# A hybrid gMLP and Mamba-2 layer on one core: small parameters, last sums, late squares and inverse roots emitted elsewhere

## The chip, the cores and the metric

One core of a Trainium2 chip. TensorE (PE) multiplies matrices into eight PSUM banks; VectorE (DVE), ScalarE (ACT) and GpSimd (POOL) do the elementwise work; the SP queue issues the loads and ACT's queue the stores. The metric is the device time of one execution in microseconds, as the median of several runs.

## The reference

One layer (DEPTH 1, batch 1, 1024 tokens, width 1024) in float32:

```python
mod = jax.nn.silu(c) @ ada_w + ada_b
shift, scale, gate = jnp.split(mod, 3, axis=-1)
h = rms_norm(x, norm_w) * (1 + scale[:, None, :]) + shift[:, None, :]
proj = h @ w_in
gm_u, gm_v, gm_z, ssm_z, xbc, dt_raw, g_a, g_b = jnp.split(proj, SPLITS, axis=-1)
y_a = spatial_gating(gelu(gm_u), gelu(gm_v), gm_ln_w, gm_ln_b, gm_ws, gm_bs) * silu(gm_z)
xbc = silu(causal_depthwise_conv(xbc, conv_w, conv_b))
xs, bm, cm = jnp.split(xbc, (SSM_D_INNER, SSM_D_INNER + SSM_GROUPS * SSM_STATE), axis=-1)
dt = softplus(dt_raw + dt_bias)
a = -jnp.exp(a_log)
y_b = ssd_scan(xs, dt, a, bm, cm) + xh * d_skip[:, None]
yz = (y_b * silu(ssm_z)).reshape(b, s, 8, 256)
y_b = rms_norm(yz, ssm_norm_w per group)
merged = sigmoid(g_a) * (y_a @ w_proj_a) + sigmoid(g_b) * (y_b @ w_proj_b)
x = x + gate * (merged @ w_out)
return rms_norm(x, final_norm_w)
```

The `rms_norm` of `yz` is what the change works on most: for each of 8 groups and 1024 tokens, the inverse root of the mean of 256 squares.

## The kernel before

**Precision and products.** Each float32 operand is split into a high part (a cast to fp32r, on ACT) and a low part (the rest, a subtraction on VectorE, names ending in l), and a product is three matmuls: high by high, high by low, low by high. The large products use a scheme with seven products of sums of blocks instead of eight (names p1 to p7; t1 to t4 and s1 to s4 are the sums).

**Stages.** 0 to 76 us: the modulation vector (`pm`, matrix-vector products with `aw` in eight steps), h (transposes `px`, then `hf`, `b11` ... `t4`) and first products (`acc`), steps n = 1 to 7 side by side. 75 to 153 us: the v projection (`v_block`), 28 units of 12 matmuls (2.72 us each). 153 to 955 us: the other columns of the in-projection in pairs (names ending in cb, uz, x, g, z), with convolution and gates. 955 to 1145 us: the SSD in four rounds of two groups (0 and 1, 2 and 3, and so on) with four steps of two chunks each, filled up with the matmuls of proj_a (`pma`, eight output blocks dd). 1157 to 1318 us: proj_b, in units p1, p3, p6, p5, p7, p2, p4 with eight k each. Then the out projection.

**Order.** Instructions under `pin` stay in program order on their engine; the others are placed by the framework's scheduler. `later(delay, f, ...)` puts a piece of work into a list, and `run_tasks` emits it that many slots on, a slot being about a product. Tiles share slots by tag: a `w4` slot (`wide`) is taken over once the tile before it has been read for the last time, and SP, like every engine, takes its instructions in order.

**Small parameters.** `late_loads` (L235) loads convolution weights and norm weights into `pkb` (five loads on SP); after product 12 of step n = 4 `small_parameters` (L453) transposes it on PE into `pp1` and copies the result on VectorE into `par2` and `cwt`, and `dsk` into `dskt`. `cwt` is first used at L1029, at 167.87 us.

**Last sums.** `last_sums` (L325) forms the sums t1, t3, t2, t4 of the last k block of h in slots 7 to 9 of step 7; `last_split` (L154) splits them for the products. PE's first operand of the v projection, `p1v0h`, is cast on ACT behind `t1h`.

**Squares and roots.** In each group the gated output `yz` is squared on ACT for the two halves q of the tokens (four chunks each), `post2` (L1222) sums the squares over channels by matmuls with `ones` (`pq`), writes mean + eps into `ssq` on VectorE and, for q = 1, takes the power -0.5 on POOL for that group; `post3` (L1237) transposes the group's roots on PE, copies them to a row (the tiles `cwt` and `tri` are used again for it) and stores them in `rs_d`, from where they come back to all partitions as `rb`. In proj_b VectorE forms `yn` = `yn` x weight x `rb` (L1535) and splits it into the operands `p1bh`, `p1bl`, `p3bh` and so on. For the last round's groups 6 and 7 and q = 1 the two squared tiles are kept (`late`), and their sums (`y0p`, `y1p`) and transposes (`y2p`, `y3p`) stand between the units k = 1, 2 and k = 4, 6 of p1, in PSUM banks that p3 takes over.

**Weights of proj_a.** `wa_block` (L1319) makes `wah` (ACT) and `wal` (VectorE) of the next block dd + 1 after k = 1 of a block.

## Time and profile before

| what | us |
|---|---|
| runs | 1399.33, 1403.52, 1399.36 (median 1399.36) |
| profiled execution, its own time | 1403.59 |
| its span | 1401.9 |
| PE busy / VectorE / ACT / POOL | 1372.1 / 1044.2 / 802.1 / 187.1 |

The page gives the span in 40 slices; a digit is the busy share of a slice in tenths, PEclk the granted clock of PE:

```profile
PE   8899999999999999999999999999999999999998
DVE  4676876777778789688888786388767755859976
ACT  5564566666656665465576565587766723223443
POOL 1000000000000000000000000028878840000002
PEclk9999999999999999999999999999999999999999
```

A row of the timeline has start, duration, engine, line, operation, out<-in, shapes, count and, in brackets, the idle time before it with what ended it. A row of the waits has the engine that waited, its line, what it waited for, and then total us, times and the longest. A row of windows has the stretch, its length, busy us of PE, PE's weight load, VectorE, ACT and POOL, then the granted clock, the DMA share and GB/s.

### The profile page before, as it was taken

Reading aid. Unit: us, or ns where it says so; the run is one execution under the profiler, and the core shown is the slowest. Engines: PE = TensorE matmul, PEld = TensorE weight load, DVE = VectorE, ACT = ScalarE, POOL = GpSimd, SP = SyncE. Lnnn points to the kernel's source line nnn. Section 1 sums busy time; section 2 is a strip of 40 time slices with the busy share of each in tenths; the row PEclk is TensorE's granted clock in tenths of the full one; section 3 lists DMA queues with packets and bytes.
Section 4 is the critical chain, followed back from the end, with each engine's and each line's share of the span. In section 5 each row is a group of like instructions: output and inputs, shape, how many; then the busy total and the mean of one; then the engine's idle time right before and its main releaser. Section 6 shows DMA issues by size and latency. Waiting matters only on the chain.

```text
span 1401.9 us, 20221 instructions
## 1 busy us (share of the span) xinstructions
PE 1372.1 (98%) x6967; PEld 1136.7 (81%) x6967; DVE 1044.2 (74%) x1725; ACT 802.1 (57%) x1447; POOL 187.1 (13%) x188
## 2 busy tenths in 40 slices
PE   8899999999999999999999999999999999999998
PEld 7578888888888888888888888888888887888886
DVE  4676876777778789688888786388767755859976
ACT  5564566666656665465576565587766723223443
POOL 1000000000000000000000000028878840000002
PEclk9999999999999999999999999999999999999999
DMA  8575533333344667786665765598777746978913
GB/s 264 164 233 153 150 120 106 105 121 120 110 131 139 199 191 238 228 265 208 199 210 169 242 217 165 169 350 310 280 255 272 279 162 240 346 251 306 384 64 120
DMA packets 247227, 288.60 MB, mean 206 GB/s; under 512 B 14508, under 2 KB 194132, under 8 KB 247124
## 3 DMA queue, kind: packets, MB, share of 16 engines
q1 hardware_dynamic: 173716, 203.76, 45.0%
q10 hardware_dynamic: 73408, 83.54, 17.6%
q8 instruction: 55, 0.90, 0.3%
q14 instruction: 48, 0.39, 0.1%
HBM read 199.79 MB, written 87.46 MB: 205 GB/s over the span
## 4 chain that ended last, share of the span: by engine, by line
PE 81%; DMA 8%; DVE 4%; ACT 3%; issue 1%; SPq 1%; POOL 1%; ACTq 0%; POOLq 0%; DVEq 0%
PE xz L571 6%; PE xx L571 6%; PE xcb L571 6%; PE xuz L571 5%; PE xg L571 5%; PE ox L1783 3%; PE yp L1597 3%; PE ycb L571 3%; PE yz L571 3%; DMA dcy<-acs_d 3%; PE vx L960 3%; PE yx L571 3%; PE pma L81 3%; PE yg L571 3%; PE yuz L571 3%; PE zz L571 2%
## 5 line engine op out<-in xcount | busy, mean ns | idle before, releaser
L1113 POOL TENSOR_SCALAR_AFFINE_SELECT dcy<-dcy 128x1024 f32<-128x1024 f32 x32 | 35.0, 1094 | 799.3 <-DMA yl<-ya_d 752.0
L1118 ACT ACTIVATE dcy<-dcy,nacs 128x128 f32<-128x128 f32 x256 | 78.5, 389 | 14.9 <-POOL dcy L1113 14.4
L1110 ACT ACTIVATE ea<-dcy 64x512 f32<-64x512 f32 x64 | 40.1, 626 | 14.3 <-DMA dcy<-acs_d 13.9
L1535 DVE SCALAR_TENSOR_TENSOR yn<-yn,par,rb 128x512 f32<-128x512 f32 x32 | 23.9, 747 | 27.5 <-DMA yn<-yb_d 27.5
L81 PE MATMUL pma<-yh,wah 128*128 128x512 f32 x128 | 43.9, 424 | 0.0
L81 PE MATMUL pma<-yh,wal 128*128 128x512 f32 x128 | 42.7, 415 | 0.0
L1138 DVE TENSOR_TENSOR dcy<-dcy,pc 128x1024 f32<-128x1024 f32 x32 | 38.9, 1217 | 4.9 <-PE pc L84 4.3
L1198 DVE TENSOR_TENSOR ym<-yn,ea 128x512 f32<-128x512 f32 (+1 forms) x32 | 19.9, 622 | 29.8 <-PE yn L81 29.6
L1200 POOL TENSOR_TENSOR yz<-y,sl 128x512 f32<-128x512 f32 x32 | 41.4, 1292 | 1.1
L81 PE MATMUL pma<-yl,wah 128*128 128x512 f32 x128 | 40.5, 398 | 0.0
L1033 ACT ACTIVATE ac<-ac 128x1024 f32<-128x1024 f32 x32 | 33.9, 1060 | 9.7 <-DVE ac L1031 9.5
L1199 POOL TENSOR_TENSOR y<-y,ym 128x512 f32<-128x512 f32 (+1 forms) x32 | 36.6, 1142 | 15.2 <-DVE ym L1198 14.7
L81 PEld LDWEIGHTS yn<-sl,st 128*128 128x128 f32 x224 | 30.3, 190 | 9.0 <-POOL yz L1220 2.4
L81 PE MATMUL yn<-sl,st 128*128 128x128 f32 x224 | 31.6, 276 | 5.5 <-DVE st L1168 5.5
L81 PE MATMUL sp<-xe,bn 128*128 128x256 f32 x112 | 33.4, 416 | 3.0 <-DVE ssq L1229 1.5
L81 PE MATMUL yi<-dcy,xd 128*64 128x128 f32 x512 | 35.9, 283 | 0.0
L1031 DVE SCALAR_TENSOR_TENSOR ac<-c2x,cwt,ac 128x1023 f32<-128x1023 f32 (+2 forms) x24 | 30.7, 1280 | 6.4 <-ACT ac L1029 6.3
L1031 DVE SCALAR_TENSOR_TENSOR ac<-c2cb,cwt,ac 128x1023 f32<-128x1023 f32 (+2 forms) x24 | 30.6, 1275 | 5.2 <-ACT ac L1029 5.1
L1166 POOL TENSOR_TENSOR st<-st,cd 128x256 f32<-128x256 f32 x48 | 33.0, 687 | 8.6 <-PE yn L81 5.7
L995 ACT ACTIVATE vm<-vm,vr 128x128 f32<-128x128 f32 x64 | 25.8, 484 | 14.2 <-DMA vm<-v_d 13.7
L830 ACT CAST wbb<-wbr 128x512 fp32r<-128x512 f32 x32 | 19.8, 619 | 23.6 <-DMA wb_d<-wbb 17.2
L1798 POOL TENSOR_TENSOR r<-r,fnw 128x512 f32<-128x512 f32 x4 | 5.3, 1344 | 205.7 <-ACT junk L1796 205.7
(2979 smaller groups left out, 4388.6 us busy)
## 6 DMA issues: line engine op xcount, KB each, us to landing
sl<-s_d SPq DMA_DIRECT2D x32, 768.0 KB
s_d<-ac ACTq DMA_DIRECT2D x32, 512.0 KB
wb_d<-wbb ACTq DMA_DIRECT2D x32, 512.0 KB
dcy<-acs_d SPq DMA_DIRECT2D x32, 512.0 KB
av<-in_w_in_dram SPq DMA_DIRECT2D x36, 256.0 KB
aw<-in_ada_w_dram SPq DMA_DIRECT2D x16, 512.0 KB
wbr<-in_w_proj_b_dram SPq DMA_DIRECT2D x32, 256.0 KB
yb_d<-yz ACTq DMA_DIRECT2D x32, 256.0 KB
```

The source lines that it names most:

```text
L81: pin(PE.matmul(acc, l, r, start=first, stop=last))
L571: pin(PE.matmul(ps, lw[:, k * P : (k + 1) * P], r[k], start=first and n + k == 0, stop=n == 2 and k == 3, skip_group_check=not first))
L960: pin(PE.matmul(ps[pn][j], l[:, j * P : (j + 1) * P], r, start=nm in ("p1", "p5", "p2") and n + units[i][1] == 0, stop=n == 2 and k == 3, ...
L1031: V.scalar_tensor_tensor(ac[:, s:], cc[:, : S - s], conv_wt[:, 3 - s, i : i + 1], ac[:, s:], op0=ALU.mult, op1=ALU.add)
L1110: A.activation(ea[hh * HD : (hh + 1) * HD], dcy.rearrange("p (j e) i l -> p e j (i l)", e=2)[hh * HD : (hh + 1) * HD, hh], AF.Exp)
L1113: G.affine_select(out=d8, in_=d8, compare_op=ALU.is_ge, fill=-1e30, base=0, pattern=[[0, 2 * HPG], [1, P]], channel_multiplier=-1)
L1118: A.activation(dcy[:, h, i, :], dcy[:, h, i, :], AF.Exp, bias=sub[:, i, h : h + 1])
L1138: V.tensor_tensor(d3, d3, pc[:, 0:256].unsqueeze(1).to_broadcast([P, HPG, 256]), op=ALU.mult)
L1199: G.tensor_add(y1[:, :, t0:], y1[:, :, t0:], m[:, :, t0:])
L1200: G.tensor_mul(yz, y1, sl[:, 4:6])
L1597: pin(PE.matmul(ps[j], a[:, v, js], r, start=first and n + k == 0, stop=n == 2 and k == KT - 1, skip_group_check=not first))
L1783: pin(PE.matmul(ps, a[:, tsl], b[:, cs], start=first and n + j == 0, stop=n == 2 and j == 3, skip_group_check=not first))
```

## The change

- The small parameters are loaded 25 slots into the pairs' list of tasks and transposed 4 slots later; `pkb` becomes a `w4` tile, zeroed on POOL.
- The sums of the last k block are formed in the v projection's units 0 to 3 and split in units 1 to 4.
- POOL's sum of two squared tiles comes 5 slots after them. For groups 6 and 7 at q = 1 the two tiles are also added on POOL, and their matmuls with `ones` stand before the last five steps of proj_a; the transposes of their roots stand after k = 1 and 2 of p1.
- The roots of groups 0 to 3 and of 4 and 5 are taken in one batch each by a first guess and three Newton steps on VectorE, two operations a slot or less (`roots`); groups 6 and 7 keep the power on POOL.
- The low parts `wal` are formed after k = 3 of a block, not k = 1.

```diff
@@ -157,6 +157,10 @@
+    def last_sum(i):
+        b11, b12, b21, b22 = (hfs[3 + 4 * (j // 2), j % 2] for j in range(4))
+        pin(V.tensor_sub(*((b11, b12, b11), (b12, b22, b12), (b22, b22, b11), (b21, b21, b22))[i]))
@@ -192,8 +196,6 @@
-        pkb = p0.tile([P, 2, P], F32, name="pkb", tag="pkb")
-        V.memset(pkb[:, 0], 0.0)
@@ -234,11 +236,6 @@
             load(wd, w_in[:, COL_DT : COL_DT + NH].rearrange("(k p) c -> p k c", p=P))
-            at = 0
-            for src, n in [(conv_b, 32), (ssm_norm_w, 16), (gm_ln_w, 8), (gm_ln_b, 8)]:
-                load(pkb[at : at + n, 0], src[0].rearrange("(r q) -> r q", q=P))
-                at += n
-            load(pkb[:, 1], conv_w[0].rearrange("k (i q) -> (k i) q", q=P))
@@ -321,17 +318,6 @@
-        def last_sums(step):
...
@@ -450,21 +436,10 @@
-        def small_parameters():
...
-            if n == KT - 1 and at in (6, 7, 8, 9):
-                (lambda: dt_products(3), *(lambda i=i: last_sums(i) for i in range(3)))[at - 6]()
+            if n == KT - 1 and at == 6:
+                dt_products(3)
@@ -488,8 +463,6 @@
-                if n == 4 and at == 12:
-                    small_parameters()
@@ -507,6 +480,27 @@
+    def small_parameters():
+
+        pkb = wide("pkb").rearrange("p (i q) -> p i q", q=P)
+        G.memset(pkb[:, 0], 0.0)
+        at = 0
+        for src, n in [(conv_b, 32), (ssm_norm_w, 16), (gm_ln_w, 8), (gm_ln_b, 8)]:
+            load(pkb[at : at + n, 0], src[0].rearrange("(r q) -> r q", q=P))
+            at += n
+        load(pkb[:, 1], conv_w[0].rearrange("k (i q) -> (k i) q", q=P))
+        later(4, small_parameters2, pkb)
+
+    def small_parameters2(pkb):
+        pp = bank("pp1")
...
@@ -961,15 +955,12 @@
-            if u == 0:
-                operands(2)
-                last_split("t2")
-            elif u == 1:
-                operands(3)
-                last_split("t3")
-            elif u == 2:
-                last_split("t4")
-                operands(4)
+            if u < 3:
+                operands(2 + u)
+            if 0 < u < 5:
+                last_split((None, "t1", "t3", "t2", "t4")[u])
+            if u < 4:
+                last_sum(u)
@@ -1209,15 +1200,15 @@
-                self.late = [turn(r, f"sq{g}", F32) for r in (y1_r, ym_r)]
-                with tc.high_priority():
-                    for j in range(2):
-                        A.activation(self.late[j], yz[:, j], AF.Square)
+                self.late = sq = [turn(r, f"sq{g}", F32) for r in (ea_r, (ym_r, y1_r)[g % 2])]
+                for j in range(2):
+                    pin(A.activation(sq[j], yz[:, j], AF.Square))
+                G.tensor_add(sq[0], sq[0], sq[1])
...
-            G.tensor_add(sq[0], sq[0], sq[1])
+            later(5, G.tensor_add, sq[0], sq[0], sq[1])
@@ -1225,14 +1216,15 @@
...
-            if q == 1:
+            if q == 1 and g > NG - 3:
                 c8 = slice(g * NCH, (g + 1) * NCH)
                 G.tensor_tensor(ssq[:, c8], ssq[:, c8], nhalf, op=ALU.pow)
-                if g < NG - 2:
-                    later(8, self.post3)
+            elif q == 1 and g in (3, 5):
+                later(1, roots, 0 if g == 3 else 4, g + 1, 0)
@@ -1243,6 +1235,25 @@
+    def roots(a, b, step):
+
+        n = (b - a) * NCH
+        v, (y, t) = ssq[:, a * NCH : b * NCH], (par[:, i * 32 : i * 32 + n] for i in range(2))
+        if step == 0:
+            V.tensor_scalar(y.bitcast(I32), v.bitcast(I32), -0.5, float(0x5F3759DF), op0=ALU.mult, op1=ALU.add)
+            V.tensor_mul(t, y, y)
+        elif step < 7:
+            if step % 2:
+                V.scalar_tensor_tensor(t, t, -0.5, v, op0=ALU.mult, op1=ALU.mult)
+                V.scalar_tensor_tensor(v if step == 5 else y, t, 1.5, y, op0=ALU.add, op1=ALU.mult)
+            elif step < 6:
+                V.tensor_mul(t, y, y)
+        if step < 5:
+            later(1, roots, a, b, step + 1)
+        else:
+            for i in range(a, b):
+                later(2 + 2 * (i - a), groups[i].post3)
@@ -1273,6 +1284,7 @@
+    later(25, small_parameters)
@@ -1321,8 +1333,12 @@
             A.copy(wh, wr)
+            was[dd].append((wh, wl, wr))
+
+    def wa_lows(dd):
+        for i, (wh, wl, wr) in enumerate(was[dd]):
             V.tensor_sub(wl, wr, f32(wh))
-            was[dd].append((wh, wl))
+            was[dd][i] = wh, wl
@@ -1422,6 +1439,8 @@
                 if k == 1 and dd + 1 < KT:
                     wa_block(dd + 1)
+                elif k == 3 and dd + 1 < KT:
+                    wa_lows(dd + 1)
@@ -1481,9 +1500,11 @@
+    draw(left[0] - 5)
+    for late in groups[NG - 2 :]:
+        late.post2(1, late.late[:1])
     room.extend(ea_r[0] + [st_r[0][1]])
     room.extend(tag for k in range(KT - 2) for tag in ya_tags[k])
-    draw(left[0] - 5)
@@ -1711,22 +1732,19 @@
-        if nm == "p1" and k in (1, 2):
-            late = groups[NG - 3 + k]
-            late.post2(1, late.late)
...
-        if nm == "p1" and k in (4, 6):
-            groups[NG - 4 + k // 2].post3()
+        if nm == "p1" and k in (1, 2):
+            groups[NG - 3 + k].post3()
```

The same change as an order of instructions. First PE in the first products, at the end of step n = 4 (`pm_724` and `pm_710` are the same matrix-vector product of step 6; `pkb` the small parameters). Before:

```order
L81 MATMUL acc_223<-b_2_636,w0h_526 128x512
L84 MATMUL pp_708<-ident,pkb 128x128 x2
L81 MATMUL acc_222<-b22h_180,w0h_588 128x512
L81 MATMUL acc_223<-b22h_180,w0h_588 128x512
L81 MATMUL pm_724<-aw_647,scz 32x256 x8
```

and now:

```order
L81 MATMUL acc_223<-b_2_629,w0h_519 128x512
L81 MATMUL acc_222<-b22h_180,w0h_581 128x512
L81 MATMUL acc_223<-b22h_180,w0h_581 128x512
L81 MATMUL pm_710<-aw_640,scz 32x256 x8
```

The transposes of `pkb` are gone from here; they now stand behind the first product of the pairs (`xcb`).

Next VectorE in the SSD's third round, around the low part `wal` of proj_a's block 6 (`ym`, `dcy`, `xd`, `xe` and `st` are the steps of a group, `par` the scratch of the Newton steps). Before:

```order
L1427 SCALAR_TENSOR_TENSOR tha_1_9696<-tha_1_9696,pma_1_9698 128x512
L1198 TENSOR_TENSOR ym_2_10138<-yn_2_10129,ea_2_9746 128x512
L1324 TENSOR_TENSOR wal_1_10271<-wa_1_9691,wah_1_10270 128x512
L1138 TENSOR_TENSOR dcy_3_9898<-dcy_3_9898,pc_3_10143 128x1024
L1134 TENSOR_TENSOR xd_3_10152<-px_3_10142,dthq 128x512
L1134 TENSOR_TENSOR xe_3_10154<-px_3_10142,dde 128x512
L1194 SCALAR_TENSOR_TENSOR y_3_10204<-sl_3_9825,dskt,yi_3_10177 128x256 x2
L1168 TENSOR_TENSOR st_2_1_10102<-st_2_1_10102,sp_2_10096 128x256
L1168 TENSOR_TENSOR st_3_0_10188<-st_3_0_10188,sp_3_10186 128x256
```

and now:

```order
L1340 TENSOR_TENSOR wal_1_10264<-wa_1_9680,wah_1_10263 128x512
L1250 TENSOR_TENSOR par<-par 128x32
L1189 TENSOR_TENSOR ym_2_10126<-yn_2_10117,ea_2_9734 128x512
L1247 SCALAR_TENSOR_TENSOR par<-par,ssq 128x32
L1129 TENSOR_TENSOR dcy_3_9886<-dcy_3_9886,pc_3_10134 128x1024
L1125 TENSOR_TENSOR xd_3_10143<-px_3_10133,dthq 128x512
L1125 TENSOR_TENSOR xe_3_10145<-px_3_10133,dde 128x512
L1248 SCALAR_TENSOR_TENSOR ssq<-par 128x32
L1159 TENSOR_TENSOR st_2_1_10088<-st_2_1_10088,sp_2_10082 128x256
L1185 SCALAR_TENSOR_TENSOR y_3_10198<-sl_3_9812,dskt,yi_3_10169 128x256 x2
L1159 TENSOR_TENSOR st_3_0_10180<-st_3_0_10180,sp_3_10178 128x256
```

`ym` has moved from ahead of `wal` to behind it, and three Newton operations stand between `wal` and the two `st`.

Last VectorE at the start of proj_b (`pq_1` are the late sums of squares of groups 6 and 7). Before:

```order
L1229 TENSOR_SCALAR ssq<-pq_0_10919 128x4
L1535 SCALAR_TENSOR_TENSOR yn_0_10970<-yn_0_10970,par_139,rb_0_10963 128x512
L1229 TENSOR_SCALAR ssq<-pq_0_10937 128x4
L1573 TENSOR_TENSOR p1bl_10984<-yn_0_10965,p1bh_10983 128x512
L1578 TENSOR_TENSOR p1a_10967<-p1r_10968,p1a_10967 128x512
```

and now:

```order
L1221 TENSOR_SCALAR ssq<-pq_0_10931 128x4
L1235 COPY tri<-pr_10941 8x128
L1221 TENSOR_SCALAR ssq<-pq_0_10953 128x4
L1221 TENSOR_SCALAR ssq<-pq_1_10979 128x4
L1221 TENSOR_SCALAR ssq<-pq_1_10986 128x4
L1556 SCALAR_TENSOR_TENSOR yn_0_10995<-yn_0_10995,par_139,rb_0_10993 128x512
L1556 SCALAR_TENSOR_TENSOR yn_0_11000<-yn_0_11000,par_139,rb_0_10993 128x512
L1594 TENSOR_TENSOR p1bl_11014<-yn_0_10995,p1bh_11013 128x512
L1599 TENSOR_TENSOR p1a_10997<-p1r_10998,p1a_10997 128x512
```

Both first `yn` now stand behind the reads of the late sums; before, one of them had run already and the other stood ahead of a sum that PE has early.

More of the change, by code (lines that the diff above doesn't have):

```diff
@@ L451, in prepare @@
             return {2: lambda: (matvec(n), transposes(n, a)), 7: second}
-        def small_parameters():
-            pp = ax("pp1")
-            for i in range(2):
-                tp(pp[:, i * P : (i + 1) * P], pkb[:, i], ident)
-            for i in range(2):
-                pin(V.tensor_copy((par2, cwt)[i], pp[:, i * P : (i + 1) * P]))
-            for hh in range(2):
-                part = slice(hh * HD, (hh + 1) * HD)
-                pin(V.tensor_copy(dskt[part, :], dsk.rearrange("p (i h) -> p i h", h=2)[part, :, hh]))
         def between(n, at):
-            if n == KT - 1 and at in (6, 7, 8, 9):
-                (lambda: dt_products(3), *(lambda i=i: last_sums(i) for i in range(3)))[at - 6]()
+            if n == KT - 1 and at == 6:
+                dt_products(3)
             elif at == 2 and n > 1:
@@ L509, in first_gate @@
         later(2 + i, store, th_d[i * P : (i + 1) * P, :], sg)
+    def small_parameters():
[9 more added lines that the diff above has]
+        pp = bank("pp1")
+        for i in range(2):
+            tp(pp[:, i * P : (i + 1) * P], pkb[:, i], ident)
+        for i in range(2):
+            V.tensor_copy((par2, cwt)[i], pp[:, i * P : (i + 1) * P])
+        for hh in range(2):
+            part = slice(hh * HD, (hh + 1) * HD)
+            V.tensor_copy(dskt[part, :], dsk.rearrange("p (i h) -> p i h", h=2)[part, :, hh])
     def first_dt():
@@ L1344, in beside @@
             wa_block(0)
+            wa_lows(0)
             for k in range(2, 6):
@@ L1713, in hybrid_kernel @@
             if nm == "p1":
-                first = {t: psb.tile([P, 512], F32, name=f"{t}p", tag=f"b{t}") for t in ('y2', 'y0', 'x0', 'x1', 'x2', 'y3', 'x3', 'y1')}
+                first = {t: psb.tile([P, 512], F32, name=f"{t}p", tag=f"b{t}") for t in ('x0', 'y2', 'y0', 'x1', 'y3', 'x2', 'y1', 'x3')}
                 psx, psy = ([first[f"{v}{j}"] for j in range(4)] for v in "xy")
-                rows_bank[0] = lambda name: psy[("pq6_1", "pq7_1", "pr6", "pr7").index(name)]
+                rows_bank[0] = lambda name: psy[2 + ("pr6", "pr7").index(name)]
             elif nm in ("p5", "p2"):
```

14 lines of the change are left out of this document (3 added, 11 removed).

## The prediction

> **What bounds the kernel now.** I read the page's head first, then what TensorE waited for, then the places of the longest waits.
>
> ```profile
> PE 1372.1 (98%) x6967; PEld 1136.7 (81%) x6967; DVE 1044.2 (74%) x1725; ACT 802.1 (57%) x1447; POOL 187.1 (13%) x188
> ```
>
> PE (TensorE) is busy for 98%: the kernel is one chain of matmuls, and a change can win only by closing PE's idle time, by avoiding the slow clock behind it, or by taking matmuls out. VectorE, at 74%, counts only where PE waits for it. The list of PE's waits (total us, times, longest us) names the stalls:
>
> ```profile
> PE yn L81 <- DVE st L1168: 5.5, 5, 2.3
> PE pm L81 <- DVE cwt L458: 3.6, 1, 3.6
> PE y3p L1597 <- DVE tri L1243: 2.7, 1, 2.7
> PE vx L960 <- ACT p1v0h L890: 1.6, 1, 1.6
> ```
>
> The second, third and fourth are what the moved pieces wait in; the first lies in the SSD, where the inverse roots are computed. The reader is to see how small the stock is: of what is left out below them, one wait in the SSD is of this size, and 3.4 us at the start, which the change leaves.
>
> **Small parameters (gain, the largest term).** The transposes of the small parameters sit between step 5's and step 6's matrix-vector products, and PE stands until VectorE has copied their result out. Timeline rows (start, duration, in brackets the idle time before) and a window (the number after the five engines is the granted PE clock, the next the DMA share):
>
> ```profile
> 40.88 1.07 PE L81 MATMUL pm<-aw,scz 128*32 128x256 f32 x16
> 47.37 1.07 PE L81 MATMUL pm<-aw,scz 128*32 128x256 f32 x16
> 56.53 1.93 PE L81 MATMUL pm<-aw,scz 128*32 128x256 f32 x16 [3.60 <-DVE cwt L458]
> 65.47 0.85 PE L81 MATMUL pm<-aw,scz 128*32 128x256 f32 x12
> 56.50:58.00 1.50, 1.47 (x16) 0.59 (x16) 0.23 (x2) 0.00 (x0) 0.00 (x0) 0.50 0.00 0
> ```
>
> The stall is 3.60. Behind it the clock is 0.50, and the step that begins at 56.53 takes 65.47 - 56.53 = 8.94 where the one from 40.88 took 6.49: another 2.45. With the transposes gone PE goes on at once, so this is worth **6.05**. What VectorE did meanwhile (the low parts of h) stays; a wait for those can take part of the stall's place, so the bounds are 2 and 6.05. I take 6.05, since the steps before this one have the same h work and no such stall.
>
> The moved part costs nothing unless its loads hold up SP's queue. They now stand there ahead of the first weights of the pairs, and they need a slot that opens when a `vc` tile has been stored:
>
> ```profile
> 25.16 1.23 SPq L90 DMA_DIRECT2D pkb<-in_conv_b_dram  x1
> 28.05 1.01 SPq L90 DMA_DIRECT2D aw<-in_ada_w_dram  x2
> 113.94 0.38 SPq L90 DMA_DIRECT2D a11cb<-in_w_in_dram  x1
> 123.71 2.36 ACTq L93 DMA_DIRECT2D v_d<-vc  x4
> 135.51 0.60 ACT L557 CAST p1cb0h<-a11cb 128x512 fp32r<-128x512 f32 x1
> 153.35 1.07 PE L571 MATMUL xcb<-b11h,p1cb0h 128*128 128x512 f32 x4
> ```
>
> The stores end their issue at 126.1; some 3 us for landing (a store issued at 1179.10 let a load go at 1182.14, below) gives 129, the five loads take 28.05 - 25.16 = 2.9, so `a11cb` goes at about 132 instead of 113.94. Its cast is at 135.51, its first matmul at 153.35: the cover is 18 us behind the cast. I take 0, with bounds 0 and 2 (ACT's queue holding other casts back). PE's two transposes (0.38) move and are not added; VectorE's copies go with them to a place where the first user comes some 10 us later. Earlier on SP, the 2.9 us taken out only help.
>
> **Last sums (gain).** The sums and the first split of the last k block move behind the start of the v projection:
>
> ```profile
> 74.71 0.68 DVE L328 TENSOR_TENSOR hf<-hf 128x512 f32<-128x512 f32 x1
> 75.43 0.62 ACT L157 CAST t1h<-hf 128x512 fp32r<-128x512 f32 x1 [1.62 <-DVE hf L328]
> ```
>
> ACT stood 1.62 us for the sum, cast `t1h`, and only then `p1v0h`, for which PE waited 1.6 (the list above). Without the sum ahead, ACT casts `p1v0h` in that idle time: **1.60** (bounds 1 and 1.60). The sums are first needed seven 12-matmul units later; VectorE has the time.
>
> **Late squares and roots of the last groups (gain).** The row `y0p<-ones,sq` is 16 passes since two tiles are summed; the change adds the tiles on POOL and issues 8, as `pq<-ones,yz` already does:
>
> ```profile
> 1162.29 1.84 PE L81 MATMUL y0p<-ones,sq 128*128 128x1 f32 x16
> 1149.10 0.95 PE L81 MATMUL pq<-ones,yz 128*128 128x1 f32 x8
> ```
>
> Two groups: 2 x (1.84 - 0.95) = **1.78**. Their transposes move from p1's k = 4 and 6 to k = 1 and 2, which ends this chain:
>
> ```profile
> 1179.10 0.29 ACTq L93 DMA_DIRECT2D rs_d<-cwt  x1
> 1182.14 0.32 SPq L90 DMA_DIRECT2D rb<-rs_d  x1
> 1186.55 0.75 DVE L1535 SCALAR_TENSOR_TENSOR yn<-yn,par,rb 128x512 f32<-128x512 f32 x1 [5.77 <-DMA yn<-yb_d]
> 1187.54 0.50 PE L1597 MATMUL y3p<-p3bh,p3a 128*128 128x512 f32 x1 [2.73 <-DVE tri L1243]
> 1187.00:1189.00 2.00, 1.46 (x5) 1.23 (x6) 1.64 (x4) 1.15 (x3) 0.00 (x0) 0.86 0.84 335
> 1189.00:1191.00 2.00, 2.00 (x6) 1.51 (x6) 0.75 (x2) 1.93 (x4) 0.00 (x0) 0.50 0.27 84
> 1191.00:1193.00 2.00, 2.00 (x9) 1.59 (x8) 0.14 (x1) 0.00 (x0) 0.00 (x0) 0.79 0.60 161
> ```
>
> PE's bank `y3p` was held by a row of inverse roots that VectorE had yet to copy (`tri`), and VectorE stood 5.77 us for loads that SP held back until the roots of another group were stored. With both rows some 13 us earlier, copy and loads are over before p3 starts. Stall 2.73; clock 2 x (0.14 + 0.50 + 0.21) = 1.70; together **4.43** (bounds 2.7 and 4.43).
>
> At p1's start the same edit costs. The 8 + 8 passes now end five pairs of matmuls ahead of p1, and VectorE reads both sums before it makes p1's operands:
>
> ```profile
> 1150.92 0.68 DVE L1573 TENSOR_TENSOR p1bl<-yn,p1bh 128x512 fp32r<-128x512 f32 x1
> 1156.39 0.62 PE L81 MATMUL pma<-yh,wal 128*128 128x512 f32 x2
> 1156.85 0.39 PE L1597 MATMUL x0p<-p1bh,p1a 128*128 128x512 f32 x1
> ```
>
> A pair takes 1156.85 - 1156.39 = 0.46, so five give 2.3 us of cover. Behind the last pass come two reads (about 0.15 each, like the small row of the next part), `yn` (0.75), ACT's casts of `p1bh` and `p1a` (about 0.6 each, like `p1cb0h`), and VectorE's two low parts (0.6 apart). First matmul: 0.3 + 0.75 + 1.2 = 2.25, just in time; the third waits for the second low part, about 0.5 longer than PE needs. Loss **0.5** (bounds 0 and 2, if `yn` also meets a late load). What was a lead of 6 us (`p1bl` at 1150.92) becomes none.
>
> **Newton batches (about even, the uncertain part).** POOL loses six powers of 1.67 us; VectorE gets 20 small operations, on 128x32 and 128x16. The nearest row is the same kind on 128x8 (0.16; I take 0.2). They land beside these rows:
>
> ```profile
> 1019.09 1.67 POOL L1233 TENSOR_TENSOR ssq<-ssq,nhalf 128x8 f32<-128x8 f32 x1
> 159.67 0.16 DVE L111 SCALAR_TENSOR_TENSOR vr<-vr 128x8 f32<-128x8 f32 x1
> 1023.06 0.41 DVE L1168 TENSOR_TENSOR st<-st,sp 128x256 f32<-128x256 f32 x1
> 1075.39 0.69 DVE L1198 TENSOR_TENSOR ym<-yn,ea 128x512 f32<-128x512 f32 x1 [0.74 <-PE yn L81]
> 1078.23 0.78 DVE L1324 TENSOR_TENSOR wal<-wa,wah 128x512 fp32r<-128x512 f32 x1 [2.15 <-ACT wah L1323]
> 1027.05 0.68 PE L81 MATMUL yn<-sl,st 128*128 128x128 f32 x4 [2.29 <-DVE st L1168]
> 1082.92 0.68 PE L81 MATMUL yn<-sl,st 128*128 128x128 f32 x4 [1.71 <-DVE st L1168]
> 1132.73 0.69 DVE L1198 TENSOR_TENSOR ym<-yn,ea 128x512 f32<-128x512 f32 x1 [3.66 <-PE yn L81]
> 1029.00:1031.00 2.00, 2.00 (x18) 1.67 (x18) 1.69 (x2) 0.41 (x2) 2.00 (x3) 0.50 0.67 270
> 1083.00:1085.00 2.00, 2.00 (x19) 1.81 (x21) 1.24 (x3) 0.00 (x0) 1.47 (x3) 1.00 1.03 400
> ```
>
> At 1075 `ym` ran ahead of the wait for `wah` (2.15). In the new order it is queued behind `wal`, with root steps around it: `ym` (0.6 of its 0.69, the rest overlaps), two steps of 0.2 and a read of 0.1 come between `wal` and the `st` for which PE waited 1.71 until 1082.92. The stall grows by about **1.1**. In the second round one `st` of 0.41 (0.35 without the overlap) at 1023.06 leaves the chain between `wal` and PE's wait, so the stall of 2.29 shrinks by **0.35**; with fewer operations of POOL beside it perhaps by 0.9. The second batch falls into the 3.66 us in which VectorE waits for PE before 1132.73. Net loss **0.75**. The clock is the open end: behind 2.29 it was 0.50 (1029 to 1031), behind 1.71 it was 1.00; where a stall crosses between, about 1.7 goes with it (priced as at `y3p`). The low weight parts and POOL's adds, emitted later, have no other effect that I see: the casts that `wal` waits for stay where they are, and a square's sum is read 12 slots after it. Bounds of this part: a gain of 2.6 (0.9 + 1.7) and a loss of 2.8 (1.1 + 1.7).
>
> The Trainium skill ("TensorE: Matmul & The Clock Gate", section "Why this matters for your kernels") says that idle gaps up to about 3 us between bursts leave the clock up. The trace does not agree: gaps of 2.29 and 2.73 us halved it. By the page the enlarged stall at 1081 would be safe and the y3p term would be its 2.73 alone; I go by the rows.
>
> **Sum.** 6.05 + 1.60 + 1.78 + 4.43 - 0.5 - 0.75 = 12.6. The profiled execution took 1403.59, so its like is about 1391.0. The runs' median is 1399.36, 4.2 below it; a saving of 12.6 puts the changed median at 1386.8: **1387**.
>
> **Rivals.** First, the SSD takes its part back: the longer stall at 1081 costs the clock too (+1.7), the one before it stays (+0.35), p1 starts 2 us late (+1.5). For it: VectorE's `st` is the releaser of all five `yn` waits. Against: it needs the clock to fall. 12.6 - 3.55 = 9: 1390.
>
> Second, another wait takes the place of `cwt`: PE stands for h's low parts at 53 and keeps the slow clock, so the first term is 2. For it: VectorE had work of its own ahead of that copy, else the wait of 3.6 would be the copy's length. Against: the steps from 40.88 and 47.37 have the same parts, and no bracket stands at the latter. 12.6 - 4 = 8.6: 1391.
>
> Third, slower: SP blocked behind the small parameters. If their slot opened late, all pair weights would stand behind them in order. It costs nothing until `a11cb` is 18 us later than estimated (the cover from 135.51 to 153.35), then one for one; to come out slower than no change by 4 us it must be 18 + 12.6 + 4 = 35 us late: 1404. Against: the slot's stores are issued by 126.1.
>
> Last, the scheduler could have undone a move; the order shows each where the code puts it.
>
> **Numbers.** Forecast 0.57, first rival 0.23, second 0.14, slower 0.04, undone 0.02 (1399). About 0.3% (4.2 us) can be told from no change, so faster means under 1395.2. The forecast and the first rival nearly all fall there, of the second most: 0.87 faster, 0.09 the same, 0.04 slower. Range: the low end has the gain of 2.6 in the roots' part (3.35 better: 1383.4); the high end has both rivals together (3.55 + 4 worse: 1394.4). 1383 to 1395.
>
> **What would show it.** Right: no `cwt`, `p1v0h` or `tri` in PE's list of waits; clock 1.0 in the first products and in p3's first unit; `yn<-st` still its first row, with the longest stall near 2.8 in the third round; a PE gap under 1 us before p1; `y0p<-ones,sq` gone, eight passes in its place. Wrong: a PE wait for casts of the pair weights before the first `xcb`, a new wait in steps 5 and 6, or a clock of 0.50 behind the third round's stall.

## The result, and the profile after

| | us |
|---|---|
| kernel before, 12 runs | median 1400.62 |
| changed kernel, 12 runs | median 1400.99 (1398.66 to 1406.03) |
| ratio | 1.0008 (95% interval 0.9995 to 1.0022) |
| profiled execution of the changed kernel | 1400.70, its span 1399.0 |

The change makes no difference that can be measured. The forecast was 1387, with a range that ended at 1395. (Of all runs in this document, two took over 2300 us, one each in experiments 6 and 9; the ratios leave them out.) The page's head, and then PE's list of waits, for the changed kernel:

```profile
PE 1369.0 (98%) x6951; PEld 1133.0 (81%) x6951; DVE 1047.7 (75%) x1744; ACT 801.8 (57%) x1447; POOL 179.9 (13%) x185
```

```profile
PE sp L81 <- DVE ssq L1221: 4.7, 2, 3.0
PE yn L81 <- DVE st L1159: 4.6, 5, 2.0
PE x0p L1618 <- ACT p1a L1598: 4.4, 1, 4.4
...
PE acc L81 <- ACT b11h L300: 0.8, 1, 0.8
```

The three waits that the change was to remove (`cwt`, `tri`, `p1v0h`) are gone, and PE has 16 matmuls less. Three others of some size have come or grown: `x0p`, the first product of p1, 4.4 us; `sp` in the scan, 3.0 at its longest; and a small one of `acc` at 36 us.

The first profile of before was 1403.59, some 3 us above the medians, so both kernels were profiled a second time, unchanged (the last two of the experiments: 1400.72 and 1399.77). Between fixed points of the program, worked out from the starts of PE's rows (us):

| stretch | before | before, again | changed | changed, again |
|---|---|---|---|---|
| start of PE's count to first `pm` | 14.40 | 13.76 | 15.19 | 14.80 |
| first `pm` to first `vx` | 62.22 | 62.40 | 56.12 | 56.92 |
| first `vx` to first `xcb` | 76.73 | 76.71 | 76.18 | 76.18 |
| first `xcb` to p1 | 1003.50 | 1002.72 | 1010.37 | 1009.26 |
| p1 to p3 | 25.76 | 25.76 | 24.91 | 24.97 |
| p3 to p6 | 26.41 | 23.60 | 22.74 | 22.46 |
| p6 to PE's end | 186.22 | 187.43 | 186.85 | 186.84 |
| sum: PE's end | 1395.24 | 1392.38 | 1392.36 | 1391.43 |

The head of the kernel gains 6.81 (first `pm` to first `xcb`), a little less than forecast. The stretch up to p1 gives it all back: 7.65 us between the second profile of before and the first of the changed kernel. And p3 to p6, the place of the `tri` stall, gains 3.67 against the first profile of before but only 0.86 against the second.

**The start of p1.** Timeline rows of the changed kernel, first SP's loads, then VectorE, ACT and PE (start, duration, in brackets the idle time before):

```profile
1150.21 0.32 SPq L90 DMA_DIRECT2D rb<-rs_d  x1
1150.62 0.38 SPq L90 DMA_DIRECT2D yn<-yb_d  x1
```

```profile
1150.17 0.16 DVE L1221 TENSOR_SCALAR ssq<-pq 128x4 f32<-128x4 f32 x1 [5.33 <-PE pq L81]
1151.06 0.16 DVE L1221 TENSOR_SCALAR ssq<-pq 128x4 f32<-128x4 f32 x1 [0.73 <-PE pq L81]
1155.81 0.75 DVE L1556 SCALAR_TENSOR_TENSOR yn<-yn,par,rb 128x512 f32<-128x512 f32 x1 [4.59 <-DMA yn<-yb_d]
```

```profile
1156.67 0.62 ACT L1593 CAST p1bh<-yn 128x512 fp32r<-128x512 f32 x1 [11.86 <-DVE yn L1556]
```

```profile
1149.19 1.84 PE L81 MATMUL pq<-ones,sq 128*128 128x1 f32 x16
...
1157.86 0.80 PE L1618 MATMUL x0p<-p1bh,p1a 128*128 128x512 f32 x1 [4.40 <-ACT p1a L1598]
```

Read them backwards. PE waits 4.40 for a cast; ACT has been idle for 11.86, so it isn't ACT; VectorE has read both late sums at 1151.06 and then stands 4.59 for the load of `yn`; and that load was issued at 1150.62, right behind `rb` at 1150.21, which is when the first eight of the sixteen passes of `pq<-ones,sq`, those over group 6, were over (VectorE's read of them is at 1150.17). Before, the same two loads stood here:

```profile
1117.16 0.57 SPq L90 DMA_DIRECT2D rb<-rs_d  x1
1132.96 0.32 SPq L90 DMA_DIRECT2D yn<-yb_d  x1
```

The reason is in the diff, in one word: `turn(r, ...) for r in (ea_r, ...)`. The kept squares of group 6 now lie in a buffer of the ring `ea_r`, and `room.extend(ea_r[0] + ...)` hands that ring's buffers to proj_b's first loads. The first `rb` takes over the buffer in which `sq6` lies, so it has to wait until PE has summed it, at the very end of proj_a, and every load of proj_b stands behind it on SP's queue, in order. That is read from the code and the rows; experiments 1 and 9 test it. Behind the gap the clock falls, too (a window; the number after the five engines is the granted PE clock):

```profile
1157.00:1159.00 2.00, 1.14 (x2) 0.58 (x2) 1.93 (x4) 1.95 (x4) 0.00 (x0) 0.50 0.95 345
1159.00:1161.00 2.00, 2.00 (x6) 1.54 (x6) 1.89 (x4) 0.07 (x1) 0.00 (x0) 0.50 1.05 405
```

p1 to p3 takes 24.91, where 25.76 less the 32 passes that left it (2 x 1.84) would be 22.08: 2.83 more. The place costs 4.40 + 2.83 = 7.23 us.

**The first products.** VectorE and ACT in the changed kernel at 35 us:

```profile
35.25 0.35 DVE L503 COPY dskt<-dsk 64x16 f32<-64x16 f32 x2 [2.50 <-DMA dsk<-in_d_skip_dram]
35.62 0.16 DVE L275 TENSOR_TENSOR md<-pm,par 128x1 f32<-128x1 f32 x1
```

```profile
36.00 0.78 ACT L300 ACTIVATE b11h<-px,md 128x512 fp32r<-128x512 f32 x1 [3.71 <-DVE md L276]
```

The copies into `dskt` are written in `small_parameters2`, among the pairs, but without `pin`. They depend on nothing that is late in the program, so the scheduler put them 115 us ahead of there, before `md`, and VectorE stands 2.50 for a load of 64 x 16 numbers whose issue was at 29.89. `md` is behind it, `b11h` behind `md`, and PE behind `b11h`: 0.76 in this profile, 2.48 in the second.

**The scan.** At 1064 us the order on VectorE has changed. The same step (VectorE, then POOL) in the changed kernel:

```profile
1063.98 0.42 DVE L1159 TENSOR_TENSOR st<-st,sp 128x256 f32<-128x256 f32 x1 [2.32 <-POOL st L1157]
1064.32 1.21 DVE L1129 TENSOR_TENSOR dcy<-dcy,pc 128x1024 f32<-128x1024 f32 x1
...
1066.05 0.68 DVE L1125 TENSOR_TENSOR xe<-px,dde 128x512 f32<-128x512 f32 x1
```

```profile
1062.27 1.09 POOL L1104 TENSOR_SCALAR_AFFINE_SELECT dcy<-dcy 128x1024 f32<-128x1024 f32 x1 [3.39 <-ACT ea L1101]
1063.33 0.61 POOL L1157 TENSOR_TENSOR st<-st,cd 128x256 f32<-128x256 f32 x1
```

and VectorE before:

```profile
1069.17 1.22 DVE L1138 TENSOR_TENSOR dcy<-dcy,pc 128x1024 f32<-128x1024 f32 x1 [0.25 <-PE pc L84]
...
1070.91 0.68 DVE L1134 TENSOR_TENSOR xe<-px,dde 128x512 f32<-128x512 f32 x1
1071.54 0.42 DVE L1168 TENSOR_TENSOR st<-st,sp 128x256 f32<-128x256 f32 x1
```

`st`, which needs POOL, stood behind `xe` and stands ahead of `dcy` now; POOL is late with it for the sake of its own step of `dcy`, and so `xe`, which PE waits for, comes some 2.3 us late. (The list names `ssq`, the operation behind `xe`, as the releaser; it ends within 0.1 us of it.) The third-round stall that the prediction watched, 1.71 for `yn`, has shrunk to 0.92.

### The profile page after: what moved, and what is told of

Read it like the earlier page. It is cut to its first block, busy times and chain, and to the rows that moved or that the text cites. A ratio compares the mean times of both kernels' runs of the same rounds, so it can differ in the third digit from the quotient of the medians.

```text
span 1399.0 us, 20207 instructions
## 1 busy us (share of the span) xinstructions
PE 1369.0 (98%) x6951; PEld 1133.0 (81%) x6951; DVE 1047.7 (75%) x1744; ACT 801.8 (57%) x1447; POOL 179.9 (13%) x185
## 4 chain that ended last, share of the span: by engine, by line
PE 78%; DMA 9%; DVE 5%; ACT 2%; issue 2%; POOL 2%; SPq 1%; POOLq 0%; ACTq 0%; DVEq 0%
PE xcb L565 6%; PE xz L565 6%; PE xx L565 6%; PE xuz L565 6%; PE xg L565 5%; PE pma L81 3%; PE ox L1801 3%; PE ycb L565 3%; PE vx L954 3%; PE yp L1618 3%; PE yz L565 3%; PE yuz L565 3%; PE yx L565 3%; PE yg L565 3%; DMA yb_d<-yz 2%
```

## The experiments

All start from the kernel before or from the changed kernel, and all times are ratios to the kernel before on the same chip, with 95% intervals. None leaves out a part of the computation.

**1. Another buffer for the first load.** The changed kernel; the first three buffers that proj_b takes over are handed out in the opposite order, so that the first `rb` gets one that is free earlier.

```diff
-    first, rest = room[:3], room[10:21]
+    first, rest = room[2::-1], room[10:21]
```

> The changed kernel with one line different: the first three slots of proj_b's rings are handed out in reverse, so that the first rb takes the slot of ea7_2 and not the one in which the squares of group 6 wait for their matmuls. Theory slot: in the changed kernel SP stood at rb<-rs_d until 1150.21, because that tile takes the slot of sq6, and all of p1's loads stood behind it; with the swap rb goes before 1135, PE's wait of 4.40 for p1a and the half clock behind it (2.6 us over p1) go, and the time is about 7 us under the changed kernel: 1394. Rival reads (the prediction's own term): VectorE's reads of the late sums hold yn back; they stay, and PE would still wait 2 us or more before p1: 1398 or above. Rival loads: the loads come in time but the transfers are the limit, and the wait moves to p1's units 1 to 4: 1398.

Measured: 0.9967 (0.9953 to 0.9981), median 1395.9. The first load goes 21 us earlier than in the changed kernel, and the wait changed its size and its name (SP's timeline and PE's waits):

```profile
1129.35 0.32 SPq L90 DMA_DIRECT2D rb<-rs_d  x1
```

```profile
PE x0p L1618 <- DVE p1bl L1594: 1.4, 1, 1.4
```

One changed index is worth 0.41% (1.0008 to 0.9967), 5.7 us, with an interval of 2.7 either way. The stretches agree: p1 to p3 takes 24.14 with no gap ahead of it, so the place costs 24.14 - 22.08 = 2.06 where it cost 7.23. What stays, a wait of 1.4, is a late load of another `yn`. On VectorE it stands ahead of `p1bl`, and the read of a late sum between them takes 0.15 and waits for nothing:

```profile
1154.47 0.75 DVE L1556 SCALAR_TENSOR_TENSOR yn<-yn,par,rb 128x512 f32<-128x512 f32 x1 [2.37 <-DMA yn<-yb_d]
1155.14 0.15 DVE L1221 TENSOR_SCALAR ssq<-pq 128x4 f32<-128x4 f32 x1
1155.21 0.68 DVE L1594 TENSOR_TENSOR p1bl<-yn,p1bh 128x512 fp32r<-128x512 f32 x1
```

The order on VectorE moved with the swap (`yn` stands ahead of the reads of the late sums here, behind them in the changed kernel). That order is not what held p1 in the changed kernel: there the reads are over at 1151.22 and the load has come only at 1155.81.

**2. to 4. The parts alone.** Three kernels, each the kernel before with one part of the change: small parameters and last sums; the late squares; the roots by Newton steps. The later `wal` and the later adds of squares on POOL are in none of them. (The edits are those of the diff above; the list that gives the products of p1 their PSUM banks was the old one in the first and the third, and the changed kernel's in the second.)

> The kernel before with the small parameters and the last sums moved, and nothing else. Theory additive: PE reaches the first xcb about 5.9 us earlier (153.35 against 147.49 in the traces) and nothing behind it is fixed in time, so the whole is kept: 1394.7. Rival given back: the SSD or proj_b wait for transfers that do not start earlier, and the time is within 2 us of before: 1399 to 1402.

> The kernel before with the late squares alone moved: added on POOL, in the slots of the ea ring, matmuls ahead of the last five steps of proj_a, transposes after k = 1 and 2 of p1; powers on POOL as before. Theory slot: the wait before p1 (4 us or more, released by the load of yn) and the half clock behind it appear here too, the waits for tri and the eight plus eight passes go; from the end of proj_a to p6 the two traces differ by +1.5, so 1402. Rival: the wait belongs to the roots or the SSD's new order and is not here: 1400.6 - 3.7 - 1.8, about 1395.

> The kernel before with the roots of groups 0 to 5 in two Newton batches on VectorE, and nothing else. Theory order: without the powers the scheduler puts st ahead of dcy in places, and PE waits for xe where it did not (3.0 us at 1064 in the changed kernel); against that, other waits shrink: from the first yn wait of the SSD to proj_a's end +0.8 between the traces, so 1401, within 2 us of before. Rival harmless: the small operations lie in idle time and POOL's 10 us of powers were off the path: 1400.6 or below. Rival costly: 1404 or above, waits for VectorE in the SSD over 12 us in all.

Measured: 0.9970 (0.9960 to 0.9981), 1.0064 (1.0052 to 1.0076) and 1.0040 (1.0026 to 1.0053), medians 1396.08, 1409.34 and 1404.83. The three together would be 0.74% slower; the change as a whole is not. Each showed a wait at p1 that is in neither kernel, or not of this size (from the three lists of PE's waits, in this order):

```profile
PE x2p L1589 <- DVE tha L1419: 1.8, 1, 1.8
```

```profile
PE x0p L1600 <- ACT p1a L1580: 13.2, 1, 13.2
```

```profile
PE x1p L1617 <- DVE tha L1447: 3.4, 1, 3.4
```

VectorE in the second of them shows why it is 13.2 and not 4.4:

```profile
1157.32 0.75 DVE L1538 SCALAR_TENSOR_TENSOR yn<-yn,par,rb 128x512 f32<-128x512 f32 x1 [4.74 <-DMA yn<-yb_d]
...
1166.62 1.28 DVE L1428 SCALAR_TENSOR_TENSOR tha<-tha,pma 128x512 f32<-128x512 f32 x2
```

The `yn` for the first operand comes at 1157.32, after a wait of 4.74 for its load, much as in the changed kernel, but `x0p` starts only at 1168.05, behind `tha`. PSUM banks go round in turn. Each part shifts the turn by a different number of tiles, and so the last two sums of proj_a (`pma`) came to lie in banks that a partial kernel gave to products needed early; VectorE empties them late, since `tha` is queued behind p1's operands. These kernels thus measured a part and a misplaced bank together, and no verdict on a part rests on them.

**5. to 7. The same with the banks put right.** One line more in each: the list of p1's products is ordered so that the banks of the last `pma` fall to products that are needed late. For the first:

```diff
-                first = {... for t in ('y2', 'y0', 'x0', 'x1', 'x2', 'y3', 'x3', 'y1')}
+                first = {... for t in ('y2', 'y0', 'x0', 'x1', 'y3', 'x2', 'x3', 'y1')}
```

> e2_front with p1's banks dealt out again: moving the transposes of the small parameters into the ring of banks shifted all later banks by one, and x2p, which p1 writes first, fell on the bank of the last pma, which VectorE clears late (PE stood 1.82 for it and p1 took 29.5 us from x0p to p3, against 25.8 in before). Now y2 and y3 lie on the two pma banks. Theory bank: no wait at x2p, p1 under 26.5 us to p3; but with p1 on time the wait for tri at p3 (2.7 and the half clock, 4.4 in all), which e2_front did not show, is back, so the time stays near e2_front's 1396. Rival: the wait at p1's start had nothing to do with the bank and stays.

> e3_late with p1's banks dealt out again (y0 and y1, which only p3 writes, on the two banks of the last pma; in e3_late x0 lay on one). Theory bank and slot: of e3_late's wait of 13.2 before p1 about 9 were the bank (x0p stood until VectorE had cleared the last pma, behind p1's operands, which were themselves late for SP's slot); the slot's 4 to 5 remain, with rb<-rs_d still issued behind 1150. Time 8 to 9 under e3_late's 1409.3: 1400.5. Rival: the bank is nothing and the loads alone make the 13: 1409.

> e4_roots with p1's banks dealt out again (y2 and y3 on the two banks of the last pma; in e4_roots x1 lay on one, and PE stood 3.37). Theory bank: that wait and the half clock behind it (about 5 us) go, and of e4_roots' +4.9 nothing is left: 1400, so the roots by themselves are even. Rival roots: the Newton batches cost in the SSD (st ahead of dcy, 3.2 us at 1068 in e4_roots) and the time stays above 1403.

Measured: 0.9959 (0.9945 to 0.9974), 1.0015 (1.0002 to 1.0027) and 1.0010 (0.9998 to 1.0022). The misplaced waits are gone. In the second, 13.2 became 4.4, the wait of the changed kernel, with the first `rb` issued as late (1154.64); so the late squares bring it on their own:

```profile
PE x0p L1600 <- ACT p1a L1580: 4.4, 1, 4.4
```

In the other two the first `rb` goes at 1111.08 and 1121.03, and `x0p` doesn't wait. So the small parameters and sums are worth 5.7 us (3.6 to 7.7), with a wait for `b11h` of 1.9 in the profile. The late squares cost 2 (0.3 to 3.8), though they take 16 passes out. The roots alone come out between no change and 3 us of loss, with waits at `sp` of 3.05 at 1068 us and 3.48 at 1098. Added up that is 0.16% faster, with an interval of about 0.23% on the sum. The whole is 0.08% slower (interval 0.14%). The two differ by no more than their intervals allow, so the parts needn't interact, but can, and the two moves that none of these kernels has may cost something as well.

**8. The copies of `dskt` pinned.** Experiment 1, and the copies held to the place where they are written:

```diff
-            V.tensor_copy(dskt[part, :], dsk.rearrange("p (i h) -> p i h", h=2)[part, :, hh])
+            pin(V.tensor_copy(dskt[part, :], dsk.rearrange("p (i h) -> p i h", h=2)[part, :, hh]))
```

> e1_swap with the two copies of dskt kept in program order, so behind the copies of par2 and cwt. Theory dskt: freed of its place, the copy was put behind b22l at about 32 us, where it waited for the load of dsk and held md, and with it h and PE (0.8 us in the changed kernel, 1.65 in e1_swap, 3.10 in e2_front); that wait goes and the time falls by 1 to 4 us under e1_swap's 1395.9: 1393.5. Rival aw: the wait is for the weights aw and only shows at dskt: no gain, 1396.

Measured: 0.9928 (0.9910 to 0.9946), median 1391.44. VectorE takes `md` at once:

```profile
32.00 0.16 DVE L275 TENSOR_TENSOR md<-pm,par 128x1 f32<-128x1 f32 x1 [0.82 <-PE pm L81]
```

No wait for `b11h` is left, and from the first `pm` to the first `xcb` PE takes 130.05, against 139.11 before and 132.30 in the changed kernel. That is 2.3 to 2.9 us for the pin (132.90 in experiment 1). The ratios, taken on two chips, put it at 5.5, with an interval of about 3 either way, which takes in the 2.9. The profiled execution is the slowest of its six (1395.96) and has a wait of 4.62 at `sp` for `bn` at 1095 us that was 0.94 in the changed kernel.

**9. The squares back in their old buffers.** The changed kernel, without the order of experiment 1; the kept squares of both groups lie in the rings of `y1` and `ym`, as before.

```diff
-                self.late = sq = [turn(r, f"sq{g}", F32) for r in (ea_r, (ym_r, y1_r)[g % 2])]
+                self.late = sq = [turn(r, f"sq{g}", F32) for r in (y1_r, ym_r)]
```

> The changed kernel with one line altered: the last two groups' squares lie in the buffers that they had in the kernel before (the rings of y and ym), not in the ring of the output staging whose slot proj_b's first rb tile takes next. Everything else of the change stays. Theory slot (the first load of proj_b waits on SP's queue for the reader of the squares, and every load of proj_b behind it): that load is issued before 1135 us again, the 4.40 us gap of TensorE ahead of p1 shrinks to at most 2.0 and the half-clocked start of p1 goes with it, so about 5 to 6 us less than the changed kernel: 1394 to 1396, ratio to before about 0.996. Rival (p1 is late because VectorE reads the late sums and the last tha product ahead of p1's operand, whatever SP does): the gap stays over 3.5 us and the time at or over 1399. In both the swap of the room's places isn't there, so a gain here is the slot's alone and not the other order's.

Measured: 1.0030 (1.0017 to 1.0044), median 1404.30: slower, where the slot theory had 0.996. The load did what the theory says (the `yn` behind it goes at 1127.74), and a new wait came in (SP's timeline, PE's waits, ACT's timeline, POOL's timeline):

```profile
1113.51 0.64 SPq L90 DMA_DIRECT2D rb<-rs_d  x1
```

```profile
PE pq L81 <- POOL sq L1206: 6.3, 1, 6.3
```

```profile
1150.52 1.15 ACT L1205 ACTIVATE sq<-yz 128x512 f32<-128x512 f32 x2 [0.16 <-PE pq L81]
```

```profile
1153.56 1.65 POOL L1225 TENSOR_TENSOR ssq<-ssq,nhalf 128x8 f32<-128x8 f32 x1 [10.47 <-DVE ssq L1221]
1155.18 1.53 POOL L1206 TENSOR_TENSOR sq<-sq,sq 128x512 f32<-128x512 f32 x1
```

The squares of group 7 now wait for PE's passes over group 6's, and POOL's add of them stands behind a power that waits for VectorE. PE stands at `pq` instead of `x0p`. So the slot's part of the theory holds (the load is early, VectorE has finished p1's first `p1bl` and `p1a` at 1150.34, before PE stops at 1150.49, and the wait at `x0p` is gone), its price forecast does not: in the change the buffer in `ea_r` also kept the two groups apart. Experiment 1 keeps that and mends the load.

**10. The roots taken out again.** Experiment 8 with the two powers on POOL for all groups, as before, and the banks put in order.

```diff
-            if q == 1 and g > NG - 3:
+            if q == 1:
...
-            elif q == 1 and g in (3, 5):
-                later(1, roots, 0 if g == 3 else 4, g + 1, 0)
+                if g < NG - 2:
+                    later(8, self.post3)
...
-                first = {... for t in ('x0', 'y2', 'y0', 'x1', 'y3', 'x2', 'y1', 'x3')}
+                first = {... for t in ('y0', 'x0', 'y2', 'x1', 'y1', 'x2', 'y3', 'x3')}
```

> The version with the other room for the first loads and the pinned dskt copies, with the Newton batches taken out again: each group's root by the two powers on GpSimd as before, the rest of the change kept, and p1's eight banks listed so that the last two sums of tha lie on the banks of y1 and y0. Theory order (the Newton batches cost about what they save, because st moves ahead of the operands xd and xe in the third round of the scan and TensorE waits some 3 us there at half clock): 0 to 3 us less than with the batches, ratio 0.990 to 0.993, the gaps of 3 us at sp in the scan's rounds three and four gone (each below 2.0). Rival (the batches are worth what the change means by them, GpSimd's powers being what held the rounds up): 2 to 4 us more than with them, ratio 0.994 to 0.996, with gaps at yn or sp that are longer than 2 us in at least two rounds.

Measured: 0.9916 (0.9900 to 0.9931), median 1388.23 in 4 runs, 11.9 us under the kernel before and the fastest of all. PE's waits:

```profile
PE yn L81 <- DVE st L1159: 5.4, 3, 2.4
...
PE sp L81 <- DVE ssq L1221: 1.5, 1, 1.5
```

The 3 us at `sp` are gone; `yn` has its 2.4 of before back. So the long `sp` stall comes with the Newton batches, and the long `yn` stall goes with them. Against experiment 8 the intervals overlap: the batches are worth nothing that these runs can tell. From first `xcb` to p1 PE takes 1004.53, which is the 1002.72 of before and about the passes that moved in (1.90); so the scan loses nothing there.

**11. and 12. Both kernels profiled again.**

> The kernel before, unchanged, profiled a second time, since its first profile was 3 to 4 us above its median. Theory (the stalls that the sum was made of belong to every execution, and the 3 us lie elsewhere): PE waits 3.6 for cwt, 2.7 for tri and 1.6 for p1v0h again, each within 0.4 us, and first vx to first xcb, first xcb to the SSD and p1 to p3 agree within 1 us. Rival (the sum was made from an execution with unusually long stalls): these three waits together come out at least 2 us smaller than 7.9.

> The changed kernel, unchanged, profiled a second time. Theory (its stalls come from the order of instructions and of loads, so they belong to every execution): the gap ahead of x0p at 4.4, the one at sp near 1064 at 3.0 and the one for b11h at 0.8, each within 0.6 us. Rival (one of them is this execution's own): it is absent or differs by more than 1.5 us.

Measured: in the kernel before, the waits for `cwt` and `p1v0h` came out alike (3.6 and 1.6), that for `tri` did not: 1.5 in place of 2.7, and with the clock up behind it. PE's waits, VectorE's timeline and a window:

```profile
PE y3p L1597 <- DVE tri L1243: 1.5, 1, 1.5
```

```profile
1184.10 0.75 DVE L1535 SCALAR_TENSOR_TENSOR yn<-yn,par,rb 128x512 f32<-128x512 f32 x1 [4.05 <-DMA yn<-yb_d]
```

```profile
1187.00:1189.00 2.00, 2.00 (x10) 1.65 (x10) 0.69 (x1) 1.49 (x3) 0.00 (x0) 1.00 0.32 93
```

VectorE waited 4.05 for the load of `yn` ahead of the copy, 5.77 in the first profile. The three waits together are 1.2 us smaller, between the two theories; with the clock, p3 to p6 is 2.81 shorter, as much as the distance between the two profiles of before (1395.24 and 1392.38 at PE's end). The two other kernels that keep the old `tri` chain and start p1 on time show the same two cases: in experiment 5 the wait is 2.95, the clock behind it 0.50 and p3 to p6 takes 26.60; in experiment 7 they are 1.69, 1.00 and 23.74. In the changed kernel the gaps at `x0p` and `sp` are 3.74 and 3.09 in the second profile (the first is 0.66 off, just more than the 0.6 expected), so both belong to it; the one for `b11h` is 2.48 instead of 0.76, so by the rival's bound its size is each execution's own: it goes with the landing of `dsk`.

## Why the prediction was wrong, step by step

The terms beside what the table of stretches shows, from the second profile of before to the first of the changed kernel:

| term | forecast | measured |
|---|---|---|
| small parameters and last sums (first `pm` to `xcb`) | -7.65 | -6.81 |
| halved passes of the late squares | -1.78 | -1.78 |
| `tri` chain (p3 to p6) | -4.43 | -0.86 |
| start of p1 | +0.5 | +7.23 |
| scan and proj_a, with the roots and `wal` | +0.75 | +1.35 |
| ahead of `pm`, and behind p6 | 0 | +1.43 and -0.58 |
| sum | -12.6 | 0.0 |

The measured +1.35 is 7.65 less the gap of 4.40 and the 1.90 of passes that moved ahead of p1 (2 x 0.95; with the 3.68 that left p1 they make the -1.78, which is thus worked out from the same rows as the forecast's and not measured apart). The +1.43 ahead of `pm` is the spread of the start: 13.76 to 15.19 in four profiles.

**Start of p1: the step that failed.** It said that VectorE "reads both sums before it makes p1's operands" and gave that 0.5, at most 2 "if `yn` also meets a late load". The order on VectorE was right, and a late load was thought of; that the load itself waits for the late sums was not. The prediction asked what is queued behind the waiting reads on VectorE, and did not ask whose buffer the kept squares sit in and who takes it next. It weighed just that question for the small parameters (its third rival, SP blocked behind a slot) and not for the squares, in the same diff. Of the measured 7.23, experiment 1 gives back 5.2 by the stretches (5.7 by the ratio), by one index in the list of buffers. Of the 2.06 that it leaves, near the upper bound of 2, 1.40 comes from what that bound named, a late load of `yn`. Against the forecast this term alone is 6.7 of the 12.6 us that are missing.

**The `tri` chain: right mechanism, size wrong.** The wait is gone, but it was sized from one execution, in which it was 2.73 with the clock halved behind it; in the other it was 1.54 at full clock. With experiments 5 and 7 the count is two of each, so a saving near the 4.43 was there in half of these executions. The text noted that the profiled execution lay 4.2 above the median, and subtracted the savings from the median all the same. Some 2.8 us of the saving were part of that distance and could not be had twice.

**Small parameters and last sums: held, less a wait that was not seen.** Stall and slow clock behind `cwt` and the wait for `p1v0h` went as forecast, and the loads that now stand ahead of the pairs' weights held up nothing: from `vx` to `xcb` PE takes 0.53 less, not more. "VectorE's copies go with them to a place where the first user comes some 10 us later" failed for `dskt`: they went to 35 us. With them pinned the two terms give 139.11 - 130.05 = 9.1, more than the forecast; no run here shows where the further 1.4 comes from.

**Late passes: held in number.** PE has 16 passes less; their price was not measured apart. **Roots: near the size forecast, by another mechanism.** That the size came out near was luck. The third-round stall at `yn`, forecast to grow by 1.1, shrank from 1.71 to 0.92; the loss came from `st` ahead of `dcy`, at a place that the prediction did not look at. That the scheduler reordered because POOL's power was gone is argued from the order; that the stall comes and goes with the batches is shown (experiments 4, 7 and 10).

**The clock.** The prediction went by the trace against the Trainium skill ("TensorE: Matmul & The Clock Gate", section "Why this matters for your kernels": gaps up to about 3 us are safe). The new gap of 3.04 at `sp` is just beyond that figure and tells little; that of 2.28 in the second profile of before halved the clock again (PE's timeline and a window):

```profile
1025.60 0.68 PE L81 MATMUL yn<-sl,st 128*128 128x128 f32 x4 [2.28 <-DVE st L1168]
```

```profile
1027.00:1029.00 2.00, 2.00 (x17) 1.67 (x17) 1.68 (x4) 0.27 (x2) 1.91 (x2) 0.50 0.88 360
```

so the rows of the scan still disagree with the Trainium skill, and the row of 2.48 us in the last section agrees with it.

**The rivals.** None was the outcome. The first (the roots take their part back and p1 starts 2 us late) named both places, each at under a third of what p1 alone cost.

**With the slips mended** (experiment 10: the other buffer, the pin, and the roots as before) the change saves 11.9 us (interval 9.7 to 14.0), near the forecast of 12.6. So the late load, the loose copies and the batches between them account for most of what was missing. That the two figures are so near is partly luck, since the terms differ.

**Still open:** whether pinning `dskt` is worth more than the stretch it acts on, what the later `wal` and the later adds on POOL do, and whether the roots are worth a microsecond either way.

## What to carry to other kernels

When a tile is kept alive longer, look up which buffer it sits in and what takes that buffer next; if that is a load at the head of an in-order queue, the price is the delay of everything behind it; one index gave back over 5 us here. An instruction that loses its `pin` in a move can travel anywhere its inputs allow, and one that waits for a load holds up what is queued behind it. Size a stall from more than one execution when the profiled one lies above the median, and when a part of a change is tried alone, see first that rotating resources (here PSUM banks) still fall as they did.

## What the runs showed of the hardware that was not expected

Gap length alone does not tell whether PE's clock falls. Behind 2.28 us in the scan it was 0.50, as the window above shows; behind 2.48 us among the first products, in the second profile of the changed kernel, it stayed up (PE's timeline and a window):

```profile
37.21 0.73 PE L81 MATMUL acc<-b11h,w0h 128*128 128x512 f32 x2 [2.48 <-ACT b11h L300]
```

```profile
39.00:41.00 2.00, 2.00 (x14) 1.79 (x15) 1.96 (x5) 1.26 (x4) 0.00 (x0) 1.00 0.42 114
```

And a small load is not a quick one: `dsk` was issued at 29.89 and its 64 x 16 numbers released VectorE only at 35.25, 5.4 us on. `yn`, issued at 1150.62, released it at 1155.81, 5.2 us on.
